# Adaptive modulation ahead of the input projections, by sets of 128 features in place of 256

## The chip, the cores and the metric

The kernel runs on one core of a Trainium2 chip. The metric is the device time of one execution in microseconds (us); the median of three runs of the kernel before is 1643.5 us (1642.47 to 1644.42). The engines are named as in the profile: PE is TensorE, DVE is VectorE, ACT is ScalarE, SP is the queue that issues most transfers.

## What is computed

The reference is one layer of a diffusion backbone over 256 latent tokens with 256 context tokens, model width 2048, float32. The change touches its first step only: both streams are normalised, scaled and shifted, with a scale and a shift per feature that are themselves the product of a vector with a weight matrix.

```python
mod = jax.nn.silu(c) @ w_mod[l] + b_mod[l]
sh_m, sc_m, ga_m, sh_f, sc_f, ga_f = [m[:, None, :] for m in jnp.split(mod, N_MOD, axis=-1)]
mod_c = jax.nn.silu(c_ctx) @ w_mod[l] + b_mod[l]
...
hc = modulate(rms_norm(xc, norm_pre_mix[l]), shc_m, scc_m)      # h * (1 + scale) + shift
pc_i, pc_ff, pc_fb = jnp.split(hc @ w_in[l][:, :3 * D_HGRN], 3, axis=-1)
...
h = modulate(rms_norm(x, norm_pre_mix[l]), sh_m, sc_m)
p_i, p_ff, p_fb, p_q, p_g, p_cv, p_cg, p_gc, p_gh = split_proj(h @ w_in[l])
```

Everything behind the projections (a gated linear recurrence, a convolution branch, a merge, a squared-ReLU MLP) is left as it was.

## The kernel before, in words

Activations are held transposed: 128 features on the partitions, tokens along the row. A **row block** k (0 to 15) is 128 of the 2048 features; `h{k}` is the modulated block of both streams, as a rounded part `hi` and a rest `lo`, since every float32 product is made of three products of such parts (`whi`, `wlo` are the parts of a weight tile). Weight tiles are 128 x 1024 (512 KB) and come through one ordered list, `Stream` (L52): `fetch_to(13)` keeps up to 13 transfers ahead, of which at most 5 are in the `raw` buffers and 8 in pages (`rawpage`). Tiles of `w_in` and the `wmd` tiles use `raw`; `wm0` tiles use pages. SP issues them strictly in the list's order, and a transfer waits for its buffer.

The scale and shift of a **set** of 256 features (two row blocks) need 16 blocks of 128 rows of `w_mod`. Twelve of them (`KP`) are multiplied on PE: six `wm0` tiles, 12 matmuls with 32 weight columns each (`s32`, the two vectors in two of them), put side by side in four column groups, 512 columns wide (L667 to L673). The other four are summed on DVE (`sums`, L635): two `wmd` tiles, eight multiply-and-sum instructions over 128 x 512 against `srow`, the two vectors spread over all partitions, then two small additions of the bias. `modulate` (L602) then copies PE's rows (ACT, `row`), turns them with four transposes on PE, adds the four groups (DVE, `cols`), adds the sums and forms `A` and `B` (L612 to L620), the factor and the offset of each feature. For each of its two row blocks ACT then writes `hi` (two activations) and rewrites `xT` (two more), and DVE subtracts to get `lo` (L629, L632). Last, `normed(c + 1)` (L549, DVE) multiplies the next set's two blocks by the inverse norms.

The loop over the eight sets (L664) writes this beside the products that use the finished blocks: `values` (L1296, 12 matmuls of 512 columns for a block, from `wi0` tiles) and `forget` (L575, six for a block, from `wf0` tiles). In both generators one step per call is written; `forget` runs one block behind, and it is put between the row copy and the transposes, and again behind these. In the first set `values_begun` (L1332) makes the first two blocks' products for the second half of the values, out of tile `wi0[8]`; the other 14 blocks of that half follow after the loop (`values(1, ...)`, L723), and then the kernel's long chain of projections. While the first set is awaited PE runs matmuls whose results nobody reads (`idle`, `warm`).

Order on the engines: a helper `issue_after` puts an instruction behind others; PE's is fixed by `pe` (L180). Within the other engines' queues the order is the program's, as a scheduler has laid it out: DVE takes `lo`, then `normed` of the next set, then that set's `sums`, then its `cols`, `A`, `B`. The splits of weight tiles (`whi` on ACT, L123; `wlo` on DVE, L126) are placed in between by `parts` (L656).

## Time and profile before

| | us |
|---|---|
| median of three runs | 1643.5 |
| the profiled execution | 1644.45 |
| its span, first to last instruction | 1642.7 |
| PE busy in the span | 1627.8 |
| DVE busy | 1163.1 |
| ACT busy | 799.9 |
| first product of a modulated block starts | 30.89 |
| first matmul behind the values (query projection) starts | 168.17 |

Times in the profile are counted from the span's start. In a row of the timeline stand start, duration, engine, line, operation, what it writes and reads, shape and count; brackets at the end give the idle time of that engine just before and what ended it. A DVE or ACT instruction's duration overlaps the start of the next one, so what an instruction costs in a queue is the distance between starts. PEld is the loading of weights into PE.

### The profile page before, as it was taken

What the parts mean: (1) busy time and instruction counts of PE and PEld (TensorE: products, weight loads), DVE (VectorE), ACT (ScalarE), POOL (GpSimd) and SP (SyncE); (2) the same over time, 40 slices, a digit from 0 to 9 for tenths busy, and PEclk for the clock granted to TensorE, in tenths of its full rate; (3) what the DMA queues carried; (4) which work ended last, traced back from release to release, by engine and by line L of the source; (5) the groups of instructions that cost most, each with busy time, mean ns of one, the idle gap of its engine ahead of it and who ended that gap; (6) DMA issues with size and microseconds to landing.
All of it is one profiled execution on the core that took longest, in us unless ns stands there. A gap on an engine that the chain in (4) does not pass through costs nothing.

```text
span 1642.7 us, 22019 instructions
## 1 busy us (share of the span) xinstructions
PE 1627.8 (99%) x8211; PEld 1359.2 (83%) x8211; DVE 1163.1 (71%) x1703; ACT 799.9 (49%) x1142; POOL 8.1 (0%) x18
## 2 busy tenths in 40 slices
PE   8999999999999999999999999999999999999998
PEld 6668888888988888888888888888888888888887
DVE  7777777778868889967887766456655665566555
ACT  6553444443554444653446665445544554346543
POOL 0000000000000000000000000000000000000000
PEclk9999999999999999999999999999999999999999
DMA  9998954444656556688887376677667667666553
GB/s 375 389 395 292 318 163 149 154 142 141 204 185 227 189 187 210 228 277 294 317 291 269 136 233 204 212 237 240 219 205 232 233 214 215 232 219 195 190 192 116
DMA packets 103771, 374.47 MB, mean 228 GB/s; under 512 B 11632, under 2 KB 12400, under 8 KB 103664
## 3 DMA queue, kind: packets, MB, share of 16 engines
q1 hardware_dynamic: 102096, 368.60, 66.4%
q0 software_dynamic: 1280, 4.21, 0.9%
q8 instruction: 64, 1.05, 0.3%
q14 instruction: 43, 0.35, 0.1%
q10 hardware_dynamic: 288, 0.26, 0.0%
HBM read 370.93 MB, written 2.10 MB: 227 GB/s over the span
## 4 chain that ended last, share of the span: by engine, by line
PE 93%; DVE 2%; DMA 2%; ACT 1%; issue 1%; SPq 0%; ACTq 0%; DVEq 0%
PE bank L185 62%; PE bank L252 18%; PE bank L254 9%; PE bank L1396 2%; DMA raw<-wpw 1%; DVE wlo L126 1%; DMA x<-ctx 1%; DMA rawpage<-wm 1%; ACT whi L123 0%; PE bank L1427 0%; PE bank L1438 0%; PE bank L1436 0%; DVE gacc L1236 0%; SPq L498 0%; PE bank L1419 0%
## 5 line engine op out<-in xcount | busy, mean ns | idle before, releaser
L126 DVE TENSOR_TENSOR wlo<-raw,whi 128x1024 fp32r<-128x1024 f32 x488 | 594.7, 1224 | 356.2 <-ACT whi L123 348.4
L123 ACT ACTIVATE whi<-raw 128x1024 fp32r<-128x1024 f32 x488 | 513.4, 1059 | 577.7 <-PE bank L185 322.9
L185 PE MATMUL bank<-whi,h 128*128 128x512 f32 x1264 | 396.6, 392 | 0.8 <-ACT h L629 0.5
L252 PE MATMUL bank<-h,whi 128*128 128x512 f32 x1280 | 322.4, 394 | 0.0
L185 PEld LDWEIGHTS bank<-whi,h 128*128 128x128 f32 x1264 | 237.3, 188 | 50.9 <-DVE h L1085 0.7
L252 PEld LDWEIGHTS bank<-h,whi 128*128 128x128 f32 x1280 | 230.7, 189 | 41.3
L185 PE MATMUL bank<-wlo,h 128*128 128x512 f32 x632 | 246.9, 391 | 0.7 <-DVE wlo L126 0.5
L185 PE MATMUL bank<-whi,hidh 128*128 128x512 f32 x503 | 195.3, 388 | 0.0
L185 PE MATMUL bank<-wlo,hidh 128*128 128x512 f32 x503 | 195.3, 388 | 0.0
L185 PE MATMUL bank<-whi,hidl 128*128 128x512 f32 x503 | 195.3, 388 | 0.0
L254 PEld LDWEIGHTS bank<-h,wlo 128*128 128x128 f32 x1280 | 174.6, 190 | 12.6
L254 PE MATMUL bank<-h,wlo 128*128 128x256 f32 x1280 | 178.5, 283 | 0.0
L185 PE MATMUL bank<-h,whi 128*128 128x512 f32 x512 | 164.7, 403 | 0.0
L185 PEld LDWEIGHTS bank<-wlo,h 128*128 128x128 f32 x632 | 118.8, 188 | 26.5 <-DVE wlo L126 2.4
L185 PEld LDWEIGHTS bank<-whi,hidh 128*128 128x128 f32 x503 | 94.5, 188 | 19.3
L185 PEld LDWEIGHTS bank<-whi,hidl 128*128 128x128 f32 x503 | 94.5, 188 | 19.2
L185 PEld LDWEIGHTS bank<-wlo,hidh 128*128 128x128 f32 x503 | 94.5, 188 | 19.2
L185 PEld LDWEIGHTS bank<-h,whi 128*128 128x128 f32 x512 | 92.1, 189 | 21.4 <-issue 5.9
L185 PE MATMUL bank<-h,wlo 128*128 128x512 f32 x256 | 100.2, 391 | 0.0
L1236 DVE SCALAR_TENSOR_TENSOR gacc<-raw,silu_c,gacc 128x1024 f32<-128x1024 f32 x60 | 76.8, 1279 | 0.0
L1249 DVE SCALAR_TENSOR_TENSOR raw<-raw,silu_row 128x1024 f32<-128x1024 f32 x64 | 76.5, 1220 | 0.0
L185 PEld LDWEIGHTS bank<-h,wlo 128*128 128x128 f32 x256 | 48.1, 188 | 10.5 <-DVE wlo L126 0.3
(246 smaller groups left out, 1363.0 us busy)
## 6 DMA issues: line engine op xcount, KB each, us to landing
raw<-w SPq DMA_DIRECT2D x256, 512.0 KB, 4.3
raw<-wi SPq DMA_DIRECT2D x172, 512.0 KB, 4.4
raw<-wmt SPq DMA_DIRECT2D x64, 512.0 KB, 4.3
raw<-wm SPq DMA_DIRECT2D x64, 512.0 KB, 4.5
rawpage<-wm SPq DMA_DIRECT2D x48, 512.0 KB, 8.8
raw<-wo SPq DMA_DIRECT2D x32, 512.0 KB, 4.7
raw<-wmd SPq DMA_DIRECT2D x16, 512.0 KB, 8.6
raw<-who SPq DMA_DIRECT2D x16, 512.0 KB, 5.1
```

The source lines that it names most:

```text
L123: kn.his.append(nc.scalar.activation(out=hi, in_=raw, func=AF.Copy))
L126: kn.los.append(nc.vector.tensor_tensor(lo, raw, hi.bitcast(F32), op=ALU.subtract))
L185: ins = fn(*args, **kw)
L252: nc.tensor.matmul(bank, w[0][:, cut(i)], x(k)[2], start=(k == 0), stop=False)
L254: nc.tensor.matmul(bank[:, T:], w[1][:, cut(i)], x(k)[0], start=False, stop=(k == nk - 1))
L1236: nc.vector.scalar_tensor_tensor(acc, raw, s, acc, op0=ALU.mult, op1=ALU.add)
L1249: nc.vector.scalar_tensor_tensor(raw, raw, 1.0, self.srow, op0=ALU.mult, op1=ALU.mult, accum_out=self.dot[:, 32 * j + b:32 * j + b + 1])
L1396: nc.tensor.matmul(ps[:, b * P:(b + 1) * P], w, r, start=True, stop=True)
```

## The change

The loop runs over 16 sets of one row block each. A set takes four tiles as before half a set did: the first two sets (`WHOLE`) take all 16 blocks of `w_mod`'s rows on PE (four pages `wms`, no sums on DVE); the other 14 take three pages `wm0` and one `wmd` tile. A matmul of the modulation is 256 columns wide in place of 512, and there are 200 of them where 96 were. There are two transposes a set, `cols` has four columns, the bias is added in other places (`bias1`), `normed` takes one block, and `sums` four instructions in place of eight. `values` and `forget` advance by one block in a set, and both are at block k - 1 while block k's set is modulated; before, set c took blocks 2c - 1 and 2c. `values_begun` moves from the first set to the second, its tile `wi0[8]` behind the second set's pages, and the splits are tied to other steps. The number of bytes and of products is unchanged.

```diff
+WHOLE = 2
...
-        for c in range(8):
-            for u in range(2):
-                st.add_whole(a["wmd"][2 * c + u])
-            for t in range(KP // 2):
-                st.add_whole(a["wm0"][KP // 2 * c + t], paged=True)
-            st.add(a["wi0"][c])
-            if c == 0 or c % 2 and c < 7:
-                st.add(a["wf0"][(c + 1) // 2])
-            if c == 0:
+        for k in range(KT):
+            if k < WHOLE:
+                for t in range(KT // 4):
+                    st.add_whole(a["wms"][KT // 4 * k + t], paged=True)
+            else:
+                st.add_whole(a["wmd"][k - WHOLE])
+                for t in range(KP // 4):
+                    st.add_whole(a["wm0"][KP // 4 * (k - WHOLE) + t], paged=True)
+            if k % 2 == 0:
+                st.add(a["wi0"][k // 2])
+            if k == 0 or k % 4 == 3 and k < KT - 1:
+                st.add(a["wf0"][(k + 1) // 4])
+            if k == 1:
                 st.add(a["wi0"][8])
...
-        def normed(c, *behind):
-            x = xT[c][:, :TW].rearrange("p (j t) -> p j t", j=2)
+        def normed(k, *behind):
+            x = block(k)
             with ExitStack() as after:
                 for ins in behind:
                     after.enter_context(self.tc.issue_after(ins.ins))
-                self.last3 = nc.vector.tensor_tensor(x, x, rrow.rearrange("p (o t) -> p o t", o=1).broadcast_to([P, 2, 512]), op=ALU.mult)
+                self.last3 = nc.vector.tensor_tensor(x, x, rrow, op=ALU.mult)
...
+        bias1 = self.cp.tile([P, KT], F32, name="bias1")
+        nc.vector.tensor_scalar(out=bias1, in0=v["bmod"][:, KT:2 * KT], scalar1=1.0, scalar2=None, op0=ALU.add)
...
-        def modulate(c, ps, part):
...
+        def modulate(k, ps, part):
+            row = self.small(T, "row")
+            with ExitStack() as after:
+                for ins in self.last2[:1] if k else ():
+                    after.enter_context(self.tc.issue_after(ins.ins))
+                self.last = nc.scalar.copy(out=row, in_=ps)
             yield
             pt = self.bank()
-            for j in range(4):
+            for j in range(2):
                 self.pe(nc.tensor.transpose, out=pt[:, j * P:(j + 1) * P], in_=row[:, j * P:(j + 1) * P], identity=v["ident"])
...
+            cols = self.small(4, "cols")
+            with ExitStack() as after:
+                if part is not None:
+                    after.enter_context(self.tc.issue_after(self.last5.ins))
+                nc.vector.tensor_reduce(cols.rearrange("p (j i) -> p j i", i=2), pt[:, :T].rearrange("p (j g f) -> p j f g", j=2, g=4)[:, :, 0:2, :],
+                                        axis=mybir.AxisListType.X, op=ALU.add)
+            a_, b_ = cols[:, 0:2], cols[:, 2:4]
+            if part is not None:
+                nc.vector.tensor_tensor(a_, a_, part[:, 0:2], op=ALU.add)
+            self.scaled = nc.vector.tensor_scalar(out=Av[:, :, k], in0=a_, scalar1=bias1[:, k:k + 1], scalar2=v["g_pm"][:, k:k + 1], op0=ALU.add, op1=ALU.mult)
+            if part is not None:
+                self.scaled = nc.vector.scalar_tensor_tensor(Bv[:, :, k], b_, v["bmod"][:, k:k + 1], part[:, 2:4], op0=ALU.add, op1=ALU.add)
+            else:
+                self.scaled = nc.vector.tensor_scalar(out=Bv[:, :, k], in0=b_, scalar1=v["bmod"][:, k:k + 1], scalar2=None, op0=ALU.add)
             yield
...
+            hp.append(self.page(F32R, f"h{k}"))
+            hi, lo = (hp[k].rearrange("p (i s t) -> p s i t", i=2, s=2)[:, n] for n in range(2))
+            x = block(k).rearrange("p (i t) -> p i t", i=2)
+            with self.tc.issue_after(self.his[-1].ins):
+                for o in (hi, x):
+                    for i in range(2):
+                        last = nc.scalar.activation(out=o[:, 1 - i], in_=x[:, 1 - i], func=AF.Identity, scale=Av[:, i, k:k + 1], bias=Bv[:, i, k:k + 1])
+            for i in range(2):
+                hparts[i].append(hp[k][:, (1 - i) * 512:(2 - i) * 512])
+            self.last2 = last, nc.vector.tensor_tensor(lo, x, hi.bitcast(F32), op=ALU.subtract)
+            yield
...
-        def sums(c, *behind):
...
+        def sums(k, *behind):
+            if k < WHOLE:
+                return None
+            part = self.cp.tile([P, 4], F32, name="part", tag="part", bufs=2)
+            st.fetch_to(FETCH)
+            w = st.whole()
+            for n in range(2):
+                s = w[:, n * 512:(n + 1) * 512]
                 for i in range(2):
...
+                    o = s if i else self.small(512, "junk")
+                    with ExitStack() as after:
+                        for ins in behind:
+                            after.enter_context(self.tc.issue_after(ins.ins))
+                        self.last5 = nc.vector.scalar_tensor_tensor(o, s, 1.0, srow[:, i * 512:(i + 1) * 512], op0=ALU.mult, op1=ALU.mult,
+                                                                    accum_out=part[:, 2 * n + i:2 * n + i + 1])
             return part
...
-        for c in range(8):
-            part = sums(c, self.last3)
-            ps = self.bank()
-            for t in range(KP // 2):
+        for k in range(KT):
+            part = sums(k, self.last3)
+            ps = self.bank()[:, :T]
+            nk = KT if k < WHOLE else KP
+            for t in range(nk // 4):
                 st.fetch_to(FETCH)
                 w = st.whole()
-                for k2 in range(2):
-                    k = 2 * t + k2
-                    g = 32 * (k % 4)
-                    self.pe(nc.tensor.matmul, ps[g:g + 32, :], s32[:, 32 * k:32 * k + 32], w[:, k2 * 512:(k2 + 1) * 512], start=(k < 4), stop=(k >= KP - 4))
-                if c == 0 and t < KP // 2 - 1:
+                for j in range(4):
+                    g, n = 32 * j, 4 * t + j
+                    self.pe(nc.tensor.matmul, ps[g:g + 32, :], s32[:, 32 * n:32 * n + 32], w[:, j * T:(j + 1) * T], start=(t == 0), stop=(t == nk // 4 - 1))
+                if k == 0 and t < nk // 4 - 1:
...
+                        self.pe(nc.tensor.matmul, idle[g:g + 32, :T], s32[:, :32], srow[:, :T], start=True, stop=True)
             st.fetch_to(FETCH)
-            mod = modulate(c, ps, part)
+            mod = modulate(k, ps, part)
             next(mod)
             copied = self.last
-            if c:
+            if k:
                 next(forget)
             else:
                 self.warm(5)
             next(mod)
-            if c:
+            if k:
                 next(forget)
             else:
                 self.warm(8)
-            parts(vq, copied, lo=[self.scaled])
+            if k % 2 == 0:
+                parts(vq, copied, lo=[self.scaled])
             next(mod)
-            if c == 0:
+            if k == 0 or k % 4 == 3 and k < KT - 1:
                 parts(fq, *self.last2)
+            if k == 1:
                 parts(vq2, *self.last2)
-            next(mod)
-            if c % 2 and c < 7:
-                parts(fq, *self.last2)
-            if c < 7:
-                normed(c + 1, *self.last2)
-            for _ in range(2 if c else 1):
+            if k < KT - 1:
+                normed(k + 1, *self.last2)
+            if k == 1:
+                vb = self.values_begun(hx, vq2.popleft())
+            else:
                 next(values)
-            for _ in range(2):
-                next(forget)
-            if c == 0:
-                vb = self.values_begun(hx, vq2.popleft())
...
+    def by_block(w):
+        n = w.shape[0] // P
+        return w.reshape(n // 4, 4, P, 2, KT, P)[:, :, :, ::-1].transpose(4, 0, 2, 1, 3, 5).reshape(-1, P, TW)
...
+        "wms": by_block(wm[:, :2 * D])[:WHOLE * KT // 4],
+        "wm0": by_block(wm[:KP * P, :2 * D])[WHOLE * KP // 4:],
+        "wmd": wm[KP * P:, :2 * D].reshape(512, 2, KT, P)[:, ::-1].transpose(2, 3, 1, 0).reshape(-1, P, TW)[WHOLE:],
```

What stands in DVE's queue from one `A` to the next, in the kernel before (`h_662` and `h_668` are row blocks 4 and 5, `xT_111` holds the next set's two blocks):

```order
L619 SCALAR_TENSOR_TENSOR A<-A,pack 128x2x2
L126 TENSOR_TENSOR wlo<-raw,whi 128x1024
L632 TENSOR_TENSOR h_662<-xT_110,h_662 128x2x256
L632 TENSOR_TENSOR h_668<-xT_110,h_668 128x2x256
L555 TENSOR_TENSOR xT_111<-xT_111,s_82 128x1024
L648 SCALAR_TENSOR_TENSOR junk,part<-raw,srow 128x512 x2
L648 SCALAR_TENSOR_TENSOR raw,part<-raw,srow 128x512 x2
L648 SCALAR_TENSOR_TENSOR junk,part<-raw,srow 128x512 x2
L648 SCALAR_TENSOR_TENSOR raw,part<-raw,srow 128x512 x2
```

After these come, in the kernel before, two small additions, `cols` and the next `A`. In the changed kernel (`h_676` is row block 4, `xT_110` holds blocks 4 and 5, and its second half is block 5, the next set):

```order
L632 TENSOR_SCALAR A<-cols,bias_167,pack 128x2
L127 TENSOR_TENSOR wlo<-raw,whi 128x1024
L647 TENSOR_TENSOR h_676<-xT_110,h_676 128x2x256
L560 TENSOR_TENSOR xT_110<-xT_110,s_82 128x512
L664 SCALAR_TENSOR_TENSOR junk,part<-raw,srow 128x512 x2
L664 SCALAR_TENSOR_TENSOR raw,part<-raw,srow 128x512 x2
L627 TENSOR_REDUCE cols<-bank 128x4
L631 TENSOR_TENSOR cols<-cols,part 128x2
L634 SCALAR_TENSOR_TENSOR B<-cols,pack,part 128x2
L632 TENSOR_SCALAR A<-cols,bias_167,pack 128x2
```

From one `A` to the next there is now one `lo` (L647), one `normed` of half the width (L560) and four sums; the whole sequence is passed once for every row block and no longer once for two. Behind blocks 3, 7 and 11 a `wlo` stands between `normed` and the sums, as before behind sets 1, 3 and 5. In the last set a `wlo` of a tile for the products behind the loop stands between `cols` and `A`.

At the start, ACT's queue of the kernel before (`h_394` and `h_408` are row blocks 0 and 1; the two `whi` in the middle are of `wf0[0]` and `wi0[8]`; `v` is what `values_begun` leaves):

```order
L605 COPY row<-bank 128x512
L123 ACTIVATE whi<-raw 128x1024
L629 ACTIVATE h_394<-xT_108,B,A 128x256 x2
L629 ACTIVATE xT_108<-xT_108,B,A 128x256 x2
L123 ACTIVATE whi<-raw 128x1024 x2
L629 ACTIVATE h_408<-xT_108,B,A 128x256 x2
L629 ACTIVATE xT_108<-xT_108,B,A 128x256 x2
L1347 COPY v_439<-bank 128x512 x2
```

The same place in the changed kernel (`h_368` and `h_439` are row blocks 0 and 1; the `whi` after each block's activations are of `wf0[0]` and then of `wi0[8]`):

```order
L617 COPY row<-bank 128x256
L124 ACTIVATE whi<-raw 128x1024
L644 ACTIVATE h_368<-xT_108,B,A 128x256 x2
L644 ACTIVATE xT_108<-xT_108,B,A 128x256 x2
L124 ACTIVATE whi<-raw 128x1024
L617 COPY row<-bank 128x256
L644 ACTIVATE h_439<-xT_108,B,A 128x256 x2
L644 ACTIVATE xT_108<-xT_108,B,A 128x256 x2
L124 ACTIVATE whi<-raw 128x1024
L1356 COPY v_450<-bank 128x512 x2
```

The split of `wi0[8]`, the weights of `values_begun`, has moved behind all four activations of row block 1; before it stood ahead of them. On PE `values_begun` (24 matmuls) stands behind the second set's transposes and ahead of the third set's modulation.

More of the change, by code (lines that the diff above doesn't have):

```diff
@@ L621, in modulate @@
-            yield
-            for k in range(2 * c, 2 * c + 2):
-                hp.append(self.page(F32R, f"h{k}"))
-                hi, lo = (hp[k].rearrange("p (i s t) -> p s i t", i=2, s=2)[:, n] for n in range(2))
-                x = block(k).rearrange("p (i t) -> p i t", i=2)
-                with self.tc.issue_after(self.his[-1].ins):
-                    for o in (hi, x):
-                        for i in range(2):
-                            last = nc.scalar.activation(out=o[:, 1 - i], in_=x[:, 1 - i], func=AF.Identity, scale=Av[:, i, k:k + 1], bias=Bv[:, i, k:k + 1])
-                for i in range(2):
-                    hparts[i].append(hp[k][:, (1 - i) * 512:(2 - i) * 512])
-                self.last2 = last, nc.vector.tensor_tensor(lo, x, hi.bitcast(F32), op=ALU.subtract)
-                yield
```

34 lines of the change are left out of this document (1 added, 33 removed).

## The prediction, before the changed kernel was run

> **What bounds the kernel now.** I read the page first, then the stage ahead of the query projection by windows, then one turn of DVE's queue in the timeline, then the waits, and last the two ends of the stage.
>
> ```profile
> span 1642.7 us, 22019 instructions
> PE 1627.8 (99%) x8211; PEld 1359.2 (83%) x8211; DVE 1163.1 (71%) x1703; ACT 799.9 (49%) x1142; POOL 8.1 (0%) x18
> ...
> 31.00:116.30 85.30, 85.06 (x446) 54.63 (x450) 66.77 (x176) 43.97 (x76) 0.00 (x0) 1.00 1.02 400
> 116.30:168.30 52.00, 52.00 (x235) 42.34 (x232) 38.23 (x65) 21.64 (x29) 0.00 (x0) 1.00 0.85 300
> 168.30:1642.70 1474.40, 1467.15 (x7363) 1244.70 (x7361) 1037.57 (x1412) 715.98 (x1007) 7.87 (x14) 1.00 0.64 213
> ```
>
> In a window's row stand its length, the busy times of PE, PEld, DVE, ACT and POOL, the granted clock, the share of the transfer engines and GB/s. PE is busy throughout, so what the change can do to the time is what it does to the moment at which PE starts the query projection, 168.17 us; PE's program behind it is the same. In the modulation (31 to 116 us) three things run at once and near their limits: PE 85.06 of 85.30 us, the transfers at 1.02, DVE 66.77. A share cannot tell which of them sets the pace. DVE's queue can:
>
> ```profile
> 58.71 0.17 DVE L619 SCALAR_TENSOR_TENSOR A<-A,pack 128x4 f32<-128x4 f32 x1
> ...
> 61.02 0.69 DVE L632 TENSOR_TENSOR h<-xT,h 128x512 fp32r<-128x512 f32 x1 [1.01 <-ACT xT L629]
> 63.00 0.69 DVE L632 TENSOR_TENSOR h<-xT,h 128x512 fp32r<-128x512 f32 x1 [1.28 <-ACT xT L629]
> 63.61 1.22 DVE L555 TENSOR_TENSOR xT<-xT,s 128x1024 f32<-128x1024 f32 x1
> 64.74 0.68 DVE L648 SCALAR_TENSOR_TENSOR junk<-raw,srow 128x512 f32<-128x512 f32 x1
> ...
> 69.64 0.16 DVE L653 TENSOR_TENSOR part<-part,pack 128x4 f32<-128x4 f32 x1
> 69.71 0.19 DVE L612 TENSOR_REDUCE cols<-bank 128x8 f32<-128x32 f32 x1
> 69.93 0.17 DVE L616 TENSOR_TENSOR A<-cols,part 128x4 f32<-128x4 f32 x1
> 70.14 0.16 DVE L619 SCALAR_TENSOR_TENSOR A<-A,pack 128x4 f32<-128x4 f32 x1
> ...
> 75.02 1.22 DVE L555 TENSOR_TENSOR xT<-xT,s 128x1024 f32<-128x1024 f32 x1
> 76.16 1.22 DVE L126 TENSOR_TENSOR wlo<-raw,whi 128x1024 fp32r<-128x1024 f32 x1
> 77.29 0.69 DVE L648 SCALAR_TENSOR_TENSOR junk<-raw,srow 128x512 f32<-128x512 f32 x1
> ...
> 82.69 0.16 DVE L619 SCALAR_TENSOR_TENSOR A<-A,pack 128x4 f32<-128x4 f32 x1
> ```
>
> This is a closed ring. `A` lets ACT write the blocks, ACT lets DVE subtract `lo`, and only behind `lo` stand `normed`, the sums and the next `A`. In the turn from 58.71 to 70.14 DVE is idle only for ACT: no transfer and no matmul is waited for. The turn is 11.43 us; one with the extra `wlo` is 12.55 (70.14 to 82.69), and the difference, about 1.13, is that `wlo` (76.16 to 77.29).
>
> ```profile
> DVE cols L612 <- PE bank L185: 4.7, 4, 2.6
> ...
> 46.16 0.16 DVE L619 SCALAR_TENSOR_TENSOR A<-A,pack 128x4 f32<-128x4 f32 x1
> 119.11 0.16 DVE L619 SCALAR_TENSOR_TENSOR A<-A,pack 128x4 f32<-128x4 f32 x1
> ```
>
> From the second set's `A` (46.16) to the eighth's (119.11) are six turns in 72.95 us; three of 11.43 and three of 12.55 make 71.94. So the ring sets the pace of the stage to about 1 us; DVE waited for PE's transposes four times in all (4.7 us), the longest in the start. The full transfers are the same pace, not the cause.
>
> **The change part by part.** The ring of the changed kernel, from the same rows. `A` to `lo`: 2.31 (58.71 to 61.02, two pairs of activations of one block). `lo` to `normed`: 0.61 (63.00 to 63.61). `normed` at half the width: 0.61, as the `lo` of the same shape. Four sums: 2.45, half of 64.74 to 69.64. `cols` to `A`: 0.42, with one instruction fewer than 69.71 to 70.14. Sum 6.40 for one row block, 12.80 for two, where before it was 11.43. The 1.37 more are: the first block's `lo`, which lay hidden while ACT wrote the second (+0.61), ACT's second entry (2 x 2.31 in place of 4.29, +0.33), a second `cols` to `A` (+0.34), `normed` in two (+0.09). Four blocks with one `wlo` take 26.73 in place of 23.98.
>
> PE's work in a set:
>
> ```profile
> 41.55 2.78 PE L185 MATMUL bank<-rawpage,s 128*32 128x512 f32 x24
> 44.26 0.73 PE L185 MATMUL bank<-h,whi 128*128 128x512 f32 x2
> 45.07 0.63 PE L185 MATMUL bank<-pack,row 128*128 128x128 f32 x4
> ...
> 170.14 0.95 PE bank L254 x8
> 171.10 1.84 PE bank L252 x8
> ```
>
> Each of the 12 matmuls shows as two passes, and four column groups run side by side, so 41.55 to 44.26, 2.71 us, are six passes of 0.43 and 0.13 around them. For a pass of 256 columns no row exists. Nearest are two forms of the long chain: 512 columns take 0.23 (1.84 by eight), 256 take 0.119 (0.95 by eight), so almost half. I take 0.22; the ends are 0.21 (exactly half) and 0.43 (no gain, if the loads of four column groups set the pace). A set of 12 then takes 6 x 0.22 + 0.13 = 1.45, the second set of 16 takes 1.9; two transposes take 0.35, a little over half of 0.63. Behind the first product PE has 14 x 1.45 + 1.9 = 22.2 us of these in place of 7 x 2.71 = 19.0, and 15 x 0.35 = 5.3 of transposes in place of 7 x 0.63 = 4.4: 4.1 us more. With 18 products of 0.227 (4.09; this figure comes out below) a set is 5.89 us of PE: half a microsecond less than the ring. So PE waits in every set, for `lo`, which stands ahead of the transposes in `forget`.
>
> [...] The rows of 0.23 and 0.119 leave 0.01 us that does not shrink, at least for matmuls with 128 weight columns; the sum stays with them.
>
> The start:
>
> ```profile
> 20.50 0.65 PE L185 MATMUL bank<-pack,r 128*128 128x128 f32 x4
> 21.08 0.62 PE L185 MATMUL bank<-rawpage,s 128*32 128x512 f32 x2
> 25.83 0.12 PEld L185 LDWEIGHTS bank<-rawpage,s 128*32 128x32 f32 x2 [0.28 <-DMA rawpage<-wm]
> 27.07 0.11 PEld L185 LDWEIGHTS bank<-rawpage,s 128*32 128x32 f32 x2 [0.26 <-DMA rawpage<-wm]
> 28.28 0.58 ACT L605 COPY row<-bank 128x512 f32<-128x512 f32 x1 [8.04 <-PE bank L185]
> 30.04 0.16 DVE L619 SCALAR_TENSOR_TENSOR A<-A,pack 128x4 f32<-128x4 f32 x1
> 30.24 1.09 ACT L629 ACTIVATE h<-xT,B,A 128x256 fp32r<-128x256 f32 x2 [0.41 <-DVE A L619]
> 30.89 0.50 PE L185 MATMUL bank<-whi,h 128*128 128x512 f32 x1 [0.47 <-ACT h L629]
> 32.22 1.99 ACT L123 ACTIVATE whi<-raw 128x1024 fp32r<-128x1024 f32 x2
> ...
> L228 ACT COPY terms<-bank x80: 348/359/380, 173.9 to 1547.0; 128x256 f32<-128x256 f32 x80
> ```
>
> A tile lands every 1.24 us (25.83 to 27.07); the first set now ends with the fourth tile of the list and no longer the eighth, so at about 22.1. PE comes later: from 21.08 it has four pages and three lots of idle matmuls, 14 passes of 0.22, to 24.2. Then 0.1, `row` at 256 columns 0.36 (as the copies of L228, which have that shape; 0.58 before), transposes 0.35, `cols` to `A`: first `A` at 25.4 in place of 30.04, first product 0.85 behind it as before, 26.3 in place of 30.89.
>
> This lead of 4.6 us is then lost. Block 0's values last to 29.6 (their `lo` comes 2.31 + 0.69 behind `A`), the second set's 16 matmuls to 31.5, its `A` falls at 32.7. ACT writes block 1 to 35.0 and only then splits `wi0[8]` (1.0, half of the 1.99 at 32.22): 36.0. DVE has `lo` from 35.0, `normed` from 35.6, its `wlo` from 36.3 to 37.5. PE, done with `forget` at 33.1, has next in its queue `values_begun`, which needs these: 4.4 us idle. Its remaining 23 matmuls end at 37.5 + 5.2 = 42.7, the third set's modulation at 44.2, copy, `forget` and transposes at 45.2, and the third set's `A` comes at 45.7. The old kernel had blocks 2 and 3 at 46.16; the new one has block 2 alone.
>
> From there 13 turns: 13 x 6.40 = 83.2, three `wlo` of 1.13 (3.4), and 1.2 for the `wlo` in front of the last `A`: 45.7 + 87.8 = 133.5, in place of 119.11. The end of the stage:
>
> ```profile
> 119.18 0.39 PE L185 MATMUL bank<-whi,h 128*128 128x512 f32 x1
> 168.17 1.98 PE L252 MATMUL bank<-h,whi 128*128 128x512 f32 x8
> ```
>
> Before, 216 products stood between these two (36 of values, 12 of `forget`, 168 of the second half of the values): 48.99 us, 0.227 each and no stall. In the changed kernel PE is through block 14 at 133.2 (`lo` of block 14 at 129.0, then 0.45 of `forget`, transposes 0.35, 0.68, values 2.72) and has 186 left, 42.2 us: 175.4. Some products of the second half stand ahead of block 15's in its queue and cover the last `A`. The query projection starts at 175.4 in place of 168.17: 7.2 us later. Transfers hide under this: a set's 4.75 tiles take 5.9 us, less than the ring. What was 1644.45 in the profiled execution becomes 1651.7; it lay 0.95 over the median, so against the median 1643.5 + 7.2 = 1650.7.
>
> Bounds: the ring by 0.2 a turn either way (2.6 us), the start by 1, the last `wlo` from 0 to 3 (its tile may land late, since its buffer is released by a `wlo` of block 14), the passes as above. Own range of this case: 1646.7 to 1655.5.
>
> **The rivals.** First, faster: the transfers pace the stage, and the ring has slack that I don't see.
>
> ```profile
> 116.25 0.14 PEld L185 LDWEIGHTS bank<-rawpage,s 128*32 128x32 f32 x4 [0.22 <-DMA rawpage<-wm]
> ```
>
> The last page was waited for here, and the transfers' share of 1.02 speaks for it. Then the end follows the last page: one tile more stands ahead of it (`wi0[7]`, +1.24), and behind it PE has 18 products fewer (block 13's, -4.1): 2.9 us faster, 1640.6. [...] Against it: 0.22 us of wait is a tie, and the turns add up without any transfer.
>
> Second, about the same: the ring as forecast, but `values_begun` doesn't wait, because the split of `wi0[8]` gets through earlier. Then the third `A` and all behind it come 4.4 us earlier: +2.8, 1646.3. Against it stands ACT's queue.
>
> Third, slower than forecast: a pass of 256 columns costs near 0.43. Decisive is 0.35: there PE's set (4.09 + 0.35 + 0.13 + 6 passes) passes the ring's mean of 6.68. At 0.43 a set is 7.2, 13 sets lose 6 more and the start's 28 passes 6: 1662.7. Against it the row of 0.119.
>
> **How the numbers follow.** Main case 0.74, first rival 0.10, second 0.09, third 0.07. A measurement of this kernel can tell about 0.2%, 3.3 us, from no change. Faster by more: 0.10 (the first rival; 1640.6 is at that border). Within: 0.10 (the second, and the main case's lower tail). Slower: 0.80. The range leaves out the first and third and reaches from 1645.5, below the second, to 1656.0.
>
> **What would show it.** Right: turns of about 6.4 us between `A`s without a wait for pages or transposes, 1.1 more behind blocks 3, 7 and 11; `lo` waits for ACT in every set; PE idle some 4 us ahead of `values_begun`; first product at 26, the query projection at 175. Wrong: `cols` waiting for transposes in most sets (PE's pace), pages waited for in every set (transfers), or a query projection ahead of 168.

## The result, and the profile after

| | before | after |
|---|---|---|
| median of four runs, us | 1643.41 (1642.47 to 1644.42) | 1655.68 (1654.45 to 1656.65) |
| profiled execution: span, us | 1642.7 | 1654.3 |
| first product of the values, us | 30.89 | 25.47 |
| query projection starts, us | 168.17 | 180.50 |

The change makes the kernel slower, by a ratio of 1.0074 (95% interval 1.0061 to 1.0086). By windows, the stage ahead of the query projection, counted from the first product, and all that follows it in the changed kernel:

```profile
25.47:180.50 155.03, 145.21 (x879) 103.79 (x879) 106.60 (x257) 66.59 (x112) 0.00 (x0) 0.98 0.88 328
180.50:1654.30 1473.80, 1466.99 (x7363) 1244.86 (x7361) 1040.69 (x1417) 717.14 (x1008) 7.88 (x14) 1.00 0.64 213
```

From the query projection on nothing has changed (1473.80 us; before, from 168.17 on, 1474.53). The stage begins 5.42 us earlier and ends 12.33 us later: it is 155.03 us long where it was 137.28, TensorE (PE) is idle for 9.8 us of it, and the granted clock, 1.00 before, averages 0.98.

One turn of DVE's queue in the changed kernel, from the timeline:

```profile
75.64 0.28 DVE L632 TENSOR_SCALAR A<-cols,bias,pack 128x2 f32<-128x2 f32 x1
75.83 1.22 DVE L127 TENSOR_TENSOR wlo<-raw,whi 128x1024 fp32r<-128x1024 f32 x1
78.07 0.69 DVE L647 TENSOR_TENSOR h<-xT,h 128x512 fp32r<-128x512 f32 x1 [1.02 <-ACT xT L644]
78.68 0.69 DVE L560 TENSOR_TENSOR xT<-xT,s 128x512 f32<-128x512 f32 x1
79.28 0.68 DVE L664 SCALAR_TENSOR_TENSOR junk<-raw,srow 128x512 f32<-128x512 f32 x1
...
81.73 0.17 DVE L627 TENSOR_REDUCE cols<-bank 128x4 f32<-128x16 f32 x1
...
82.14 0.28 DVE L632 TENSOR_SCALAR A<-cols,bias,pack 128x2 f32<-128x2 f32 x1
```

The ring of the prediction is there link by link: `A`, the low part 2.43 us later, `normed`, four sums, `cols`, the next `A` at 82.14. The turn is 6.50 us, and the only wait is that for ACT. From the `A` of block 2 (48.51) to that of block 14 (129.91) are twelve turns, nine of 6.50 and three of 7.63 behind blocks 3, 7 and 11. The waits in that stretch:

```profile
ACT h L644 <- DVE A L632: 38.1, 12, 4.2
DVE h L647 <- ACT xT L644: 19.0, 12, 2.1
PEld bank L186 <- DVE h L647: 7.9, 10, 1.5
PE bank L186 <- DVE h L647: 4.7, 10, 1.2
```

In each turn ACT waits for `A` and DVE for ACT, and in ten of the twelve PE waits for a low part (`h` of DVE). No page of weights and no transpose is waited for.

The start, from the timelines of PE and of DVE, and windows of 2 us:

```profile
32.14 0.40 PE L186 MATMUL bank<-h,wlo 128*128 128x512 f32 x1
35.62 0.51 PE L186 MATMUL bank<-whi,h 128*128 128x512 f32 x1 [3.08 <-ACT whi L124]
37.13 0.79 PE L186 MATMUL bank<-wlo,h 128*128 128x512 f32 x1 [1.01 <-DVE wlo L127]
...
45.44 1.50 PE L186 MATMUL bank<-rawpage,s 128*32 128x256 f32 x24
```
```profile
48.09 0.17 DVE L627 TENSOR_REDUCE cols<-bank 128x4 f32<-128x16 f32 x1 [8.57 <-PE bank L186]
```
```profile
34.00:36.00 2.00, 0.39 (x1) 0.19 (x1) 1.35 (x3) 1.56 (x3) 0.00 (x0) 1.00 1.03 404
36.00:38.00 2.00, 0.99 (x3) 0.77 (x3) 2.00 (x4) 0.00 (x0) 0.00 (x0) 0.58 1.01 403
38.00:40.00 2.00, 2.00 (x6) 1.52 (x6) 1.52 (x6) 0.00 (x0) 0.00 (x0) 0.50 1.05 412
40.00:42.00 2.00, 2.00 (x7) 1.50 (x6) 0.00 (x0) 0.59 (x1) 0.00 (x0) 0.50 1.00 401
42.00:44.00 2.00, 2.00 (x8) 1.62 (x7) 0.00 (x0) 0.59 (x1) 0.00 (x0) 0.72 1.05 418
44.00:46.00 2.00, 2.00 (x19) 1.24 (x21) 0.00 (x0) 1.10 (x2) 0.00 (x0) 1.00 1.01 401
```

PE stands idle for 3.08 and 1.01 us ahead of the values' products, for the split of `wi0[8]`. Right behind it the granted clock, the third column from the right, reads 0.58, 0.50, 0.50 and 0.72 before it is back at 1.00. So the 23 products from 37.13 on end at 45.44, after 8.31 us, and DVE waits 8.57 us for what follows them. This was not in the forecast.

The end of the stage, from ACT's and DVE's timelines:

```profile
135.98 1.06 ACT L124 ACTIVATE whi<-raw 128x1024 fp32r<-128x1024 f32 x1 [3.13 <-DMA raw<-wi]
```
```profile
136.02 0.17 DVE L627 TENSOR_REDUCE cols<-bank 128x4 f32<-128x16 f32 x1
137.07 1.23 DVE L127 TENSOR_TENSOR wlo<-raw,whi 128x1024 fp32r<-128x1024 f32 x1 [0.88 <-ACT whi L124]
138.22 0.15 DVE L631 TENSOR_TENSOR cols<-cols,part 128x2 f32<-128x2 f32 x1
...
138.42 0.28 DVE L632 TENSOR_SCALAR A<-cols,bias,pack 128x2 f32<-128x2 f32 x1
```

The last `A` would have been ready at about 136.4; in DVE's queue the `wlo` of a late tile stands in the middle of its four instructions, and it comes at 138.42, 8.51 us after the one before it.

### The profile page after: what moved, and what is told of

Its sections match the earlier page's. It is cut to its first block, busy times and chain, and to the rows that moved or that the text cites. A ratio compares the mean times of both kernels' runs of the same rounds, so it can differ in the third digit from the quotient of the medians.

```text
span 1654.3 us, 22431 instructions
## 1 busy us (share of the span) xinstructions
PE 1631.4 (99%) x8403; PEld 1365.3 (83%) x8403; DVE 1162.1 (70%) x1710; ACT 801.5 (48%) x1150; POOL 8.1 (0%) x18
## 4 chain that ended last, share of the span: by engine, by line
PE 90%; DVE 5%; ACT 2%; DMA 1%; issue 1%; SPq 0%; ACTq 0%; DVEq 0%
PE bank L186 59%; PE bank L253 18%; PE bank L255 9%; PE bank L1405 2%; ACT h L644 1%; DVE wlo L127 1%; DVE raw L664 1%; DVE junk L664 1%; ACT xT L644 1%; DMA x<-ctx 1%; DVE xT L560 0%; PE bank L1436 0%; ACT whi L124 0%; DVE h L647 0%; PE bank L1447 0%
```

## The experiments

My theory at this point: the time is lost in three places of the stage, the idle gap with the slow clock behind it, the ring's turn, and the last `wlo`. The rival: the transfers or PE set the pace, and these are only where the waiting shows. Each experiment keeps all of the kernel's work and changes its order, or adds work that nobody uses; the last changes the form of one instruction. The figure to watch beside the time is the distance between the `A`s. In the table `A`(k) is the `A` of block k. The moment of the first product differs between executions by more than an edit explains (24.65 to 27.08 us in these runs), so distances are compared rather than moments.

| run | `A`(1) to `A`(2), us | `A`(2) to `A`(14), us | projection starts | median, us | ratio to before (95%) |
|---|---|---|---|---|---|
| after | 16.42 | 81.40 | 180.50 | 1655.68 | 1.0074 (1.0061 to 1.0086) |
| gap filled | 13.93 | 81.39 | 177.01 | 1654.07 | 1.0061 (1.0046 to 1.0076) |
| split early | 10.60 | 81.39 | 173.93 | 1650.63 | 1.0042 (1.0027 to 1.0057) |
| sums early | 15.46 | 71.54 | 173.16 | 1648.29 | 1.0026 (1.0015 to 1.0036) |
| extra DVE work | 16.06 | 89.71 | 189.76 | 1664.43 | 1.0122 (1.0105 to 1.0139) |
| split and sums early | 12.98 | 71.68 | 168.46 | 1646.35 | 1.0018 (1.0009 to 1.0027) |
| the same, gaps filled | 12.95 | 71.60 | 167.74 | 1644.71 | 1.0007 (0.9998 to 1.0016) |
| three edits of order | 10.60 | 71.61 | 164.94 | 1640.92 | 0.9984 (0.9975 to 0.9992) |

**The gap filled.** In the loop over the sets, ahead of the values' first products:

```diff
             if k == 1:
+                self.warm(26)
                 vb = self.values_begun(hx, vq2.popleft())
```

> The changed kernel with 26 unused products put in ahead of the values' products, at the place where TensorE stands idle for 3.08 and 1.01 us; nothing else differs. My theory is that this idle time is what lowers the granted clock to 0.50 just behind it, and that the values' products take 8.3 us for that instead of about 5.2: with TensorE kept busy the clock stays at 1.00, A of block 2 stands at about 45.5 us in place of 48.51, everything behind it is earlier by the same 3 us, and the time is about 1653. A rival holds that the clock is not granted by what TensorE did just before, or that something else (the loads, DVE) paces the blocks behind: then nothing changes, 1655 to 1656.

PE's timeline of this kernel, and a window's row of the stretch that had 0.50:

```profile
31.57 3.01 PE L186 MATMUL bank<-ones_r 128*128 128x128 f32 x26
34.81 0.51 PE L186 MATMUL bank<-whi,h 128*128 128x512 f32 x1 [0.23 <-ACT whi L124]
36.33 0.50 PE L186 MATMUL bank<-wlo,h 128*128 128x512 f32 x1 [1.01 <-DVE wlo L127]
...
42.14 1.50 PE L186 MATMUL bank<-rawpage,s 128*32 128x256 f32 x24
```
```profile
38.00:40.00 2.00, 2.00 (x9) 1.27 (x9) 0.72 (x4) 1.17 (x2) 0.00 (x0) 1.00 1.03 404
```

The same products in the same order now take 5.81 us (36.33 to 42.14) in place of 8.31, at a clock of 1.00, and `A`(1) to `A`(2) is shorter by 2.49: the slow clock costs 2.5 us, and it is the idle time that brings it, since 26 products that nobody uses take it away. A gap of 1.01 us alone, which is still there, does not: the six rows from 34 to 46 us all read 1.00. The blocks behind are earlier by what the start gained, which the rival denies. The median fell by 1.6 us, less than the 3.5 us of the profiled execution, of which 0.8 is an earlier first `A`; the intervals of the two ratios overlap, so the size rests on the trace.

**The split early.** In the same loop:

```diff
             if k % 2 == 0:
                 parts(vq, copied, lo=[self.scaled])
+            if k == 1:
+                parts(vq2, copied, lo=[self.scaled])
             next(mod)
...
-            if k == 1:
-                parts(vq2, *self.last2)
```

> The changed kernel with the split of wi0[8] put ahead of block 1's activations on ACT, so that the values' products no longer wait for it; the same work otherwise. My theory: the gap of 3.08 and 1.01 us goes and with it the lowered clock, so that A of block 2 stands at 41 to 42 us in place of 48.51, and the time falls by 6 to 7 us to about 1649. If block 1's activations are then late by the 2 us that the split takes on ACT, the fall is 4 to 5 us. A rival, that the blocks are paced by the loads of wi0 and wi1 and would wait later for what they gain here, gives less than 2 us.

PE's timeline ahead of the values' products:

```profile
31.70 0.39 PE L186 MATMUL bank<-whi,h 128*128 128x512 f32 x1
33.01 0.50 PE L186 MATMUL bank<-wlo,h 128*128 128x512 f32 x1 [0.93 <-DVE wlo L127]
```

The gap shrinks to 0.93 us, the clock stays at 1.00, and `A`(1) to `A`(2) is 10.60 us, shorter by 5.8: 2.5 of clock and 3.3 of waiting. `A`(2) stands at 42.01, as expected, and the median is 5.05 us lower, where 6 to 7 were expected. The turns behind it are still 6.50: the blocks follow the start at the ring's pace, and the rival, that the loads would take the gain back, falls.

**The sums early.** In the list of loads, in `modulate` and in the loop:

```diff
-                st.add_whole(a["wmd"][k - WHOLE])
                 for t in range(KP // 4):
                     st.add_whole(a["wm0"][KP // 4 * (k - WHOLE) + t], paged=True)
+            if WHOLE <= k + 1 < KT:
+                st.add_whole(a["wmd"][k + 1 - WHOLE])
...
+            with ExitStack() as after:
+                if k + 1 in begun:
+                    after.enter_context(self.tc.issue_after(self.last5.ins))
-            self.last2 = last, nc.vector.tensor_tensor(lo, x, hi.bitcast(F32), op=ALU.subtract)
+                self.last2 = last, nc.vector.tensor_tensor(lo, x, hi.bitcast(F32), op=ALU.subtract)
...
-            part = sums(k, self.last3)
+            part = begun.get(k)
...
+            if WHOLE <= k + 1 < KT:
+                begun[k + 1] = sums(k + 1, self.scaled)
             next(mod)
```

> The changed kernel with the adding up of the next set's modulation put on DVE right behind this block's A and B, ahead of the low parts; the same work otherwise. My theory is that the turn of 6.50 us is a closed ring over ACT and DVE, A, h, low part, normed, sums, A. With the sums beside ACT's h the ring is about 1.2 to 2 us shorter, and the turn is set by TensorE's own 5.9 us for a set or by the ring's 5.3 us, whichever is longer: 12 turns shorter by 0.5 to 0.6 us each, so that A of block 15 stands 6 to 8 us earlier than 138.42, and the time is 1648 to 1650. The rival, that the loads or TensorE already set the turn, gives turns of 6.50 as before and a time within 1 us of 1656.

DVE's timeline in one turn, and the window from `A`(2) to `A`(14):

```profile
61.08 0.28 DVE L633 TENSOR_SCALAR A<-cols,bias,pack 128x2 f32<-128x2 f32 x1
61.27 0.68 DVE L668 SCALAR_TENSOR_TENSOR junk<-raw,srow 128x512 f32<-128x512 f32 x1
...
64.86 0.68 DVE L651 TENSOR_TENSOR h<-xT,h 128x512 fp32r<-128x512 f32 x1
65.46 0.68 DVE L561 TENSOR_TENSOR xT<-xT,s 128x512 f32<-128x512 f32 x1
66.62 0.17 DVE L628 TENSOR_REDUCE cols<-bank 128x4 f32<-128x16 f32 x1 [0.48 <-PE bank L186]
...
67.04 0.28 DVE L633 TENSOR_SCALAR A<-cols,bias,pack 128x2 f32<-128x2 f32 x1
```
```profile
49.16:120.70 71.54, 71.54 (x530) 50.05 (x529) 61.94 (x178) 38.03 (x69) 0.00 (x0) 1.00 0.97 382
```

With four instructions moved, each turn is 5.96 us (61.08 to 67.04), the ones with a `wlo` too, and what DVE waits for has changed: no longer ACT, but PE's transposes, 0.48 us here and 9.2 us over the twelve turns. PE is busy for 71.54 of 71.54 us. So the 6.50 was the ring's and nothing else's, and 5.96 is PE's own work for a set, forecast at 5.89. `A`(1) to `A`(2) is 1.0 us shorter as well, because the clock came back sooner: it reads 0.61 and 0.54 in two windows of 2 us and then 1.00, and the 23 products take 7.14 us. The twelve turns gained 9.9 us, more than the 6 to 8 that I expected, because I had not counted that the three `wlo` disappear in the wait as well. The last `A` falls 9.7 us earlier (128.70), the query projection 7.3 (173.16) and the median 7.4: the other 2.4 us are in the tail behind the last `A`, 44.5 us long in place of 42.1, since PE, now busy throughout, still has that much work queued there.

**More work on DVE.** In `normed`:

```diff
+                if behind:
+                    more = nc.vector.tensor_tensor(self.small(512, "junk"), x, rrow, op=ALU.mult)
+                    after.enter_context(self.tc.issue_after(more.ins))
                 self.last3 = nc.vector.tensor_tensor(x, x, rrow, op=ALU.mult)
```

> The changed kernel with one more multiplication of 128x512 elements on DVE, whose result nobody uses, ahead of each block's normed from block 1 on: 15 times about 0.61 us of DVE, which is idle for well over that in every turn. If the turn is a closed ring through DVE, as I hold, each turn of 6.50 us becomes 7.1, and the time rises by 13 to 15 times 0.61, that is by 8 to 9 us to about 1664. If TensorE or the loads set the turn, the addition is hidden in DVE's idle time and the time stays within 1 us of 1656.

DVE's timeline of one turn:

```profile
79.34 0.28 DVE L635 TENSOR_SCALAR A<-cols,bias,pack 128x2 f32<-128x2 f32 x1
...
81.77 0.69 DVE L650 TENSOR_TENSOR h<-xT,h 128x512 fp32r<-128x512 f32 x1 [1.01 <-ACT xT L647]
82.37 0.69 DVE L561 TENSOR_TENSOR junk<-xT,s 128x512 f32<-128x512 f32 x1
83.09 0.69 DVE L563 TENSOR_TENSOR xT<-xT,s 128x512 f32<-128x512 f32 x1
...
86.56 0.28 DVE L635 TENSOR_SCALAR A<-cols,bias,pack 128x2 f32<-128x2 f32 x1
```

The added instruction takes 0.72 us (82.37 to 83.09) and the turn grows from 6.50 to 7.22 (79.34 to 86.56); the three with a `wlo` grow by 0.60. The median rose by 8.75 us, as expected. DVE has 1.01 us of idle time in the turn, and not a tenth of a microsecond of it could take the addition in: it lies at another place of the ring.

**The same addition in the kernel before.** There, with `x[:, 0]` for `x`, ahead of each `normed` from the second set on.

> The kernel before with one more multiplication of 128x512 elements on DVE, whose result nobody uses, ahead of each set's normed from the second set on: seven of them, 0.61 to 0.72 us each. The prediction held that the old kernel's turn of 11.43 us for two blocks was a closed ring through DVE without slack; then seven turns are longer by that and the time rises by 4.3 to 5.0 us to about 1648. The rival reads the same stretch by its other full resources, TensorE busy for 72.77 of 73.00 us and the transfers at 1.02: if one of these sets the old pace and the ring only keeps step with it, the addition is absorbed and the time stays within 1 us of 1643.5.

Three of the `A`s in its DVE timeline, and the window of the same six turns in the kernel before:

```profile
58.74 0.17 DVE L622 SCALAR_TENSOR_TENSOR A<-A,pack 128x4 f32<-128x4 f32 x1
...
70.90 0.17 DVE L622 SCALAR_TENSOR_TENSOR A<-A,pack 128x4 f32<-128x4 f32 x1
...
121.55 0.17 DVE L622 SCALAR_TENSOR_TENSOR A<-A,pack 128x4 f32<-128x4 f32 x1
```
```profile
46.16:119.11 72.95, 72.72 (x386) 46.70 (x385) 58.44 (x161) 36.66 (x64) 0.00 (x0) 1.00 1.01 399
```

Median 1645.79 us, ratio 1.0012 (1.0003 to 1.0021): 2.0 us more, between the two expectations. The bare turn went from 11.43 to 12.16 (58.74 to 70.90), by all of the addition. But the six turns together grew by 3.0 us (75.96 in place of 72.95), since three of them had held up to half a microsecond of other waits that the addition displaced; and of these 3.0 us only 1.6 reached the query projection (123.62 us behind the first of these `A`s, 45.59 to 169.21, in place of 122.01). So the old ring had next to no slack in its turns, and PE, busy for 72.72 of those 72.95 us, still had products queued up behind the last `A`. That PE counts as busy hides one thing, which stands in the waits of the kernel before from 25 to 165 us:

```profile
PEld bank L185 <- DMA rawpage<-wm: 4.7, 10, 1.1
```

Ten times the loading of weights waited for a page, 4.7 us in all; four of the six modulations in those turns last 3.14 to 3.86 us, where one without a wait (at 41.55) takes 2.78. Ring, PE and transfers were tied; the prediction called the ring alone the pace.

**Split and sums early together.** Both edits, with the split's `wlo` behind the third set's sums (`lo=[self.last5]`).

> The changed kernel with both edits together, the split of wi0[8] ahead of block 1's activations and the sums ahead of the low parts; the same work otherwise. If the gap ahead of the values' products and the ring were all that the change lost, TensorE is busy from the first product (25.5 to 26 us) to the query projection. Its work there is 137.3 us in the kernel before (30.89 to 168.17) and 4.1 us more by the forecast's sum, 141.4, so the projection starts at about 167.5 and the time is about 1643, the same as before. The rival, that the transfers (at 1.02 to 1.03 of their time in both single edits) are late once the blocks come at 5.9 us, lets the clock and the ring be mended and still loses 1 to 5 us to loads: 1644 to 1648, with waits for pages or for wi0 in every other set. A faster time than before by over 0.2% (below 1640) would mean that TensorE's added work is smaller than I hold.

1646.35 us, 3 us above the 1643 that I expected and within what the rival gave. The two gains add up only in part: the sums now stand ahead of the split's `wlo` on DVE, and PE's gap ahead of the values' products is 1.00 and 2.10 us again. No page of weights was waited for, but one late load did cost time: ACT waited 2.36 us for the tile whose split stands ahead of block 14's activations, and PE then 1.16 us for block 14. The profiled execution was the fastest of eleven (1644.00 us, a mean clock of 0.999); the others scatter up to 1649.86, all at 0.997 and 0.998. Whether the gap's clock was behind that is what the next run asks.

**The same with the gaps filled**, by the `self.warm(26)` of the first experiment.

> The changed kernel with the split of wi0[8] and the sums early, as in the run of both edits, and 26 unused products ahead of the values' products, in the gaps of 1.00 and 2.10 us that were left there. In the profiled execution of both edits the clock stayed at 1.00 over these gaps and the time was 1644.0, but the median of its executions was 1646.35 at a mean clock of 0.997 to 0.998. My theory: in most of those the two gaps did lower the clock, for about 2 to 3 us; with the gaps filled the median falls to 1644 to 1645 at a clock of 0.999. The rival: the clock of those executions was lowered elsewhere, in the 1470 us behind this stage, or the scatter has nothing to do with the clock; then the median stays at 1646 to 1647.

1644.71 us, and eleven executions within 1644.16 to 1646.01, all at a clock of 0.999 or 1.000: 1.6 us less in the median and a third of the scatter, as my theory has it. The intervals of the two ratios overlap (1.0009 to 1.0027 and 0.9998 to 1.0016), the two kernels ran on different chips, no trace shows one of the longer executions, and the longest, 5.9 us above the fastest, lost more than the 2.5 us that the clock is shown to cost. So this supports the theory without proving it.

**Three edits of order.** From the kernel with both edits (no gaps filled) the third set's sums go back to their old place and the load of `wi0[8]` ahead of theirs, and the split that stood ahead of block 14 on ACT goes behind it. The change in the list of loads is left out here:

```diff
...
-            if WHOLE <= k + 1 < KT:
+            if WHOLE < k + 1 < KT:
                 begun[k + 1] = sums(k + 1, self.scaled)
-            if k % 2 == 0:
+            if k % 2 == 0 and k < KT - 2:
                 parts(vq, copied, lo=[self.scaled])
             if k == 1:
-                parts(vq2, copied, lo=[self.last5])
+                parts(vq2, copied, lo=[self.scaled])
             next(mod)
+            if k == KT - 2:
+                parts(vq, *self.last2)
```

> The changed kernel with three edits of order, the same work otherwise: the sums early from the fourth set on, the third set's at their old place; the split of wi0[8] early, its load ahead of that of the third set's sums; and the split of wi0[7], the last one ahead of block 14, behind block 14's activations on ACT. By my theory TensorE's gap ahead of the values' products falls from 3.1 to about 1 us, so that the clock stays at 1.00 in all executions, and the wait of 1.2 us ahead of the last block goes: the query projection starts at 166 to 167.5 us and the time is 1641 to 1643.5. That is bounded from below by TensorE's own work of about 141.4 us behind the first product at 24.7 (166.1). The rival, that the transfers are then late for the blocks, gives waits for pages at 60 to 120 us and a time of 1643.5 to 1647.

Windows of this kernel, of the whole stage and of the twelve turns:

```profile
24.98:164.94 139.96, 139.04 (x878) 101.85 (x879) 109.15 (x261) 68.08 (x113) 0.00 (x0) 1.00 0.95 368
42.19:113.80 71.61, 71.61 (x530) 50.06 (x529) 61.97 (x178) 37.09 (x68) 0.00 (x0) 1.00 1.03 409
```

1640.92 us, 0.9984 of the kernel before (0.9975 to 0.9992): it is faster than both, and a little below the 1641 to 1643.5 that I expected. The gap is 0.92 us, the last turn 6.53, and PE waits for nothing in between. The stage is 2.7 us longer than before (139.96 against 137.28) and begins 5.9 us earlier, so the query projection starts 3.2 us earlier. The transfers, at 1.03 over the twelve turns, just keep up: no engine waits for one there. It ends 1.2 us ahead of my floor of 166.1: I had held that PE's work adds 4.1 us to the old stage, and the stage is only 2.7 us longer. Two things in the traces bear on it. The sum took transposes by their durations, 0.35 us for two and 0.63 for four; between starts two take 0.14 (30.96 to 31.10 here) and four 0.38 (45.07 to 45.45 before), which takes about 1.4 us off the 4.1. And the old stage's 137.28 us contain the waits for pages, of which this kernel has none from `A`(2) on. How the two share the difference is not shown.

Nor is it shown how much of the gain is due to the smaller sets: the kernel before was not run with its own sums moved ahead. Its six turns are 12.16 us on average, and PE needs less for a set of 256 where it hardly waits for a page, 11.63 us from the modulation at 65.09 to that at 76.72; so the order alone might gain there too.

**The form of `A`.** In `modulate` of the changed kernel:

```diff
-            self.scaled = nc.vector.tensor_scalar(out=Av[:, :, k], in0=a_, scalar1=bias1[:, k:k + 1], scalar2=v["g_pm"][:, k:k + 1], op0=ALU.add, op1=ALU.mult)
+            self.scaled = nc.vector.scalar_tensor_tensor(Av[:, :, k], a_, bias1[:, k:k + 1], v["g_pm"][:, k:k + 1].broadcast_to([P, 2]), op0=ALU.add, op1=ALU.mult)
```

> The changed kernel with A formed by a scalar_tensor_tensor, with the bias as its one per-partition scalar and the gain as a broadcast tensor, in place of a tensor_scalar with two per-partition scalars; the same numbers come out. If the 0.28 us of that instruction is due to its form, A takes 0.16 to 0.21 us now and every turn of 6.50 us is 0.07 to 0.12 shorter, 6.38 to 6.43. If A is dear because of what it reads or where it stands, it stays at 0.28 and the turn at 6.50. The time moves by at most 1.5 us, which one look cannot tell; the turn can.

Its row in DVE's timeline:

```profile
80.56 0.22 DVE L632 SCALAR_TENSOR_TENSOR A<-cols,bias,pack 128x2 f32<-128x2 f32 x1
```

`A` takes 0.22 us in place of 0.28 and the turns are 6.43 and 6.44. The form accounts for 0.06 of the 0.10 us by which the ring was longer than forecast, a little under the range I gave. The time was 1653.96 us, in one run.

## Why the prediction was right in kind and 5.1 us short

Forecast were 7.2 us more for the start of the query projection, measured 12.3. The time, 1655.68 us, lies 0.2 above the case's own bound, 1655.5, and 0.3 inside the 1656.0 of the final range, a margin that no term of the prediction accounts for: that it lies inside is luck. The bound that was too narrow is "the start by 1": block 2's `A` came at 48.51 in place of 45.7. Point by point:

- **The ring sets the pace of the changed kernel: right.** Moved sums shorten each turn, added work lengthens a bare one by its full 0.72 us, an earlier start moves all blocks alike. Its bare length was 6.50 in place of 6.40: `A` takes 0.28 us where I had priced it at 0.16, from a row of another form. Over the twelve turns that is 1.2 us.
- **PE's work for a set is below the ring: right.** 5.96 us when the ring is out of the way, forecast 5.89. That the two are so close is in part luck: two transposes take 0.14 us in place of 0.35, and the eighteen products what is left, 4.39 in place of 4.09. The modulation's passes of 256 columns came as taken, by PE's timeline:

```profile
51.40 1.50 PE L186 MATMUL bank<-rawpage,s 128*32 128x256 f32 x24
52.83 0.72 PE L186 MATMUL bank<-h,whi 128*128 128x512 f32 x2
```

  1.43 us from one to the next, forecast 1.45. The third rival is refuted.
- **The early start is lost ahead of `values_begun`: right, and more than lost.** The wait was forecast at 4.4 us and is 3.08 and 1.01. The second rival, that it would not wait, is thereby refuted; the run with the split early made that case come true, and the time fell.
- **The step that failed:** "Its remaining 23 matmuls end at 37.5 + 5.2 = 42.7". I priced them at full clock right behind an idle time of 4.4 us that I had worked out myself in the sentence before. The clock was 0.50 there and they took 8.31 us. The run with the gap filled gives 2.5 us for it, half of the miss; at full clock they still took 5.81 us, 0.6 more than priced, for a reason that no run isolates. The idle time came as gaps of 3.08 and 1.01 us with one product between them, the product still at full speed (0.51 us); in windows of 0.5 us the clock reads 0.50 from 36.5 us on, inside the second gap. The second gap is not needed, as PE's timeline of the kernel with the other form of `A` shows:

```profile
34.90 0.80 PE L186 MATMUL bank<-whi,h 128*128 128x512 f32 x1 [3.02 <-ACT whi L124]
```

  There the first product already takes 0.80 us. In the run with more work on DVE the clock is low as well, 0.66 on average from 35 to 45 us. How long the low clock lasts differs between the runs: the window rows come to about 6.8 us at 0.50 in the changed kernel (the four rows below 1.00 fall short of it by 1.70 in all; in windows of 2 us, at a loss of 0.50, that is 6.8 us) and 3.4 in the run with the sums early. A gap of about 1 us alone left the clock at 1.00: 1.01 us with the gap filled, 0.93 with the split early, 0.92 with the three edits of order. So did the 1.00 and 2.10 us in the profiled execution with both edits.
- **The last `wlo`: right in kind, too small.** 2.0 us over a bare turn, forecast 1.2: the tile came late, ACT waited 3.13 us for it, and DVE another 0.88 for ACT. The range had 0 to 3 for it.
- **The rest.** The tail behind the last `A` is 42.1 us, forecast 41.9; `A`(1) came 0.6 us earlier than forecast. Together: 3.4 from `A`(1) to `A`(2), 1.2 in the turns, 0.9 at the last `A`, 0.2 in the tail, less the 0.6, are 5.1.
- **What bounded the kernel before: half right.** Its turn was the ring's, but PE and the transfers were as close: with its six turns lengthened by 3.0 us the projection loses 1.6, and the pages that the prediction called "the same pace, not the cause" were waited for by PE's loading of weights. For the forecast this made no difference, since the new ring is well above PE's work.
- **The first rival, transfers that pace the stage: refuted for this kernel.** No page is waited for, and with the ring opened the same transfers carried a turn of 5.96 us. Its number, 1640.6, is nearly what the last variant reaches, but by other means: PE sets the pace there.

With the right order the changed kernel is faster than the one before. The smaller pieces went with a shorter time only when they were also put in the right order: 1655.68 us as the change has them, 1640.92 with three edits of order; what the smaller pieces gave of that and what the order is not separated.

## What to carry to other kernels

Where a result must travel over two in-order queues before the next piece can begin, halving the pieces doubles the number of round trips: here two of 6.50 us stand where one of 11.43 did. Sum one round trip from the timeline's rows, and take out of it what doesn't need its result, before making the pieces smaller; the sums taken out brought the turn from 6.50 to 5.96 us. Price what follows a wait of PE and not only the wait: behind gaps of 3.08 and 1.01 us the clock read 0.50, and 23 products took 8.31 us that took 5.81 with the longer gap filled. Idle time inside a ring was no reserve for work at another place of it: one added instruction cost its full 0.72 us in a bare turn in which DVE was idle for 1.01 us, while three `wlo` that cost 1.13 us each in the ring no longer show once the sums are out of it. A busy share near 100% doesn't say that an engine sets the pace: PE was busy for 72.72 of 72.95 us of the kernel before, and its loading of weights waited 4.7 us for pages. Look for that too.

## What the runs showed of the hardware

- PE's clock in the changed kernel: 0.50 for about 6 us of work (from 37.13 us to about 43.1), behind idle times of 3.08 and 1.01 us. With the other form of `A` the first product behind a single gap of 3.02 us already took 0.80 us, in place of 0.51. Behind a single gap of 0.92 to 1.01 us, in three runs, the clock stayed at 1.00. With 26 unused products in the gap, 3.01 us of them, it stayed at 1.00 too.
- PE counted as busy for 72.72 of 72.95 us of the kernel before, while four of the six modulations in it took 3.14 to 3.86 us in place of 2.78, and the loading of weights waited for a page ten times from 25 to 165 us, 4.7 us in all.
- The DVE instruction that forms `A` took 0.28 us on 128x2 elements as a tensor_scalar with two per-partition scalars (75.64 in the changed kernel), 0.22 as a scalar_tensor_tensor with one (80.56 with the other form of `A`), and 0.16 or 0.17 in the kernel before, on 128x4, with a constant (70.14, 58.71).
